# The recurrence of a hybrid encoder layer as one stream per pair of heads, with PSUM laid out by phase

## The chip, the cores and the metric

The kernel runs on one core of a Trainium2 chip. The metric is the device time of one execution in microseconds. The engines are TensorE (PE; its weight loads are shown apart as PEld), VectorE (DVE), ScalarE (ACT), GpSimd (POOL) and SyncE (SP), which issues the DMAs. Each runs its own instructions in order; semaphores order the engines against each other.

## What is computed

One layer of a streaming encoder on 2048 prompt rows and 32 sample rows of 1024 features. After a LayerNorm, one projection yields the inputs of two branches: A, softmax attention over a band of 9 chunks of 64 frames (8 heads of 64), and B, a gated delta rule (8 heads of 64). Both are gated, projected, merged and projected once more, with a LayerNorm at the end. The change lies in branch B. Per head, with chunks of 64 tokens:

```
k_beta = kb * beta                        # a depthwise conv, SiLU and L2 norm stand before
m      = (k_beta kb^T) * decay * strict   # 64 x 64, for each chunk
t_inv  = inverse(eye + m)                 # triangular
u, w   = t_inv (v * beta), t_inv (k_beta * exp(gc))
qk     = (qb kb^T) * decay
for each chunk, in order:                 # the recurrence: s is the 64 x 64 state
    v_new = u - w s
    o     = (q * exp(gc)) s + qk v_new
    s     = s * exp(g_last) + (k * exp(g_last - gc))^T v_new
```

All but the loop can be done for any chunk at any time; the loop is sequential in the chunks of one head and independent from head to head. The sample rows are one more chunk per head, with a state of their own.

## The kernel before

The prompt is done in two halves of 1024 rows. Each half has a phase B (delta rule, function `phase_b`) and a phase A (attention, `phase_a`); the merge of both branches and the output projection come last. Two heads are one *pair* (128 partitions), so there are four pairs; a *block* is 8 chunks of one pair, so each half has 8 blocks (two per pair), and the second half one more for the sample rows.

The program is written out by a small planner (`Flow`). Each piece of work is a Python generator, a *stream*, with a clock of its own. The planner always continues the stream with the earliest clock, writes its next instructions into the engines' queues and moves the clock on by a price for each (`Engine.price`). Buffers are `Gate`s that a stream waits for and gives back. So the order of instructions on each engine is fixed when the program is built, and on the chip each engine works through its queue in that order and waits on semaphores where something is late.

TensorE's main work are the *projection jobs* (`multiply`, PSUM tag `pj`): 128 output columns of the big projection each, as three float16 products per 128 rows of input (`hi` and `lo` parts). They go on through all phases. Their order is a list: `HEAD` jobs for the merge gates, the jobs of phase B (`ORDER`, with `FILL` gate jobs between pairs), six `TAIL` gate jobs, then the jobs of phase A. A job of phase A can begin only when phase B of its half is `done`.

In phase B each block goes through these streams:

- `prep` and `system` (the stream `local` does the blocks in order): decay factors, products `k k^T` and `q k^T`, into block-diagonal tiles `k_bd`, `qk_bd`; 4 slots (`par_slots`).
- `side`: `q_bd`, `kd_bd` and the values by token, `v_t`; 3 slots each (`side_slots`, `vt_slots`).
- `solve` (two of them): 31 steps of forward substitution on VectorE (tiles `sys_t`, `sys_u`), with the data re-laid through DRAM buffers `pd` and `ud`.
- `inverse`: joins the 32 x 32 inverses to the block-diagonal `u_bd` (3 slots, `u_slots`), with one PSUM bank `a` and one `b`. With its two last copies `u_bd<-b` and `u_bd<-a`, and `side` done, the block is `ready`.
- `chain` (lines 1254 to 1293): one stream that does all blocks of the half in order, 8 steps a block. A step is the product of `k_bd` with the state (`xs`), `r` on VectorE, the product with `u_bd` (`ys`), `vn` on VectorE, the product with `kd_bd` (`ds_`), the state's update on VectorE; and for the output (`os_`) the products of `q_bd` with the state and of `qk_bd` with `vn`, copied to `v_t` by ScalarE. It gives back the slots of `par`, `side` and `u` at the block's end.
- `tail`: norm of the output, transposes, gate, to DRAM. It gives `v_t` back. The last tail ends the phase.

PSUM has 8 banks: `pj` 2, `a` 3, `b` 2, `c` 1, for the whole kernel. `chain` takes `a` banks for `xs`, `ys` and `os_` one by one and `c` for `ds_`; `inverse` and `tail` take `a` too.

Of the kernel before, what the change touches and what calls it, by code (L numbers as in the profile page):

```python
# [21 lines left out]
P = 128  # L22
# [8 lines left out]
HD = 64  # L31
# [50 lines left out]
class Gate:  # L82
# [169 lines left out]
def trunk(ctx: ExitStack, tc: tile.TileContext, x_p, x_s, cache_k, cache_v, st_conv, st_gdn,  # L252
# [23 lines left out]

    def mark():
        return Mark(flow)
# [5 lines left out]
    banks = {"pj": 2, "a": 3, "b": 2, "c": 1}  # L284
    bank = {k: gate(n) for k, n in banks.items()}

    def pt(tag):

        return psum.tile([P, 512], F32, tag=tag, bufs=banks[tag], name=tag)
# [449 lines left out]
    def phase_b(half):  # L739

        stack = ExitStack()
        bp = stack.enter_context(tc.tile_pool(name=f"bp{half}", bufs=1, reuse_waits="tile"))
# [28 lines left out]
        pd = [dram.tile([32, 1024], F32, name=f"sol_p{half}{i}") for i in range(NSIDE)]  # L771
        ud = [dram.tile([32, 1024], F32, name=f"sol_u{half}{i}") for i in range(NSIDE)]
# [41 lines left out]
        par_slots, side_slots, u_slots = gate(NPAR), gate(NSIDE), gate(NSIDE)  # L814
        e_slot, tail_slot, p_slots, vt_slots = gate(1), gate(2), gate(NSIDE), gate(NSIDE)
# [177 lines left out]
        def prep():  # L993
            yield decay_done
            for k in order:
# [24 lines left out]
                k.sc = bp.tile([P, 4, 8], F32, tag="sc", bufs=7, name="sc")  # L1020
# [46 lines left out]
        def side(k, ss):  # L1067
# [5 lines left out]
            yield side_slots  # L1073
            k.qb, k.kdb = q_bd[k.n % NSIDE], kd_bd[k.n % NSIDE]
# [27 lines left out]
            yield vt_slots  # L1102
            k.v_t = bp.tile([P, 8, HD], F32, tag="v_t", bufs=NSIDE, name="v_t")
# [17 lines left out]
        def system(k):  # L1121
# [3 lines left out]
            yield par_slots  # L1125
            yield k.qk_ready
            yield k.prep
            yield p_slots
            kb, qkb = k.kb, k.qkb = k_bd[k.n % NPAR], qk_bd[k.n % NPAR]
            p_c = k.p_c = bp.tile([P, 8, HD], F32, tag="p_c", bufs=NSIDE, name="p_c")  # L1130
# [4 lines left out]
            ss = bp.tile([P, 2, 8], F32, tag="ss", bufs=6, name="ss")  # L1135
            k.rr = bp.tile([P, 8], F32, tag="rr", bufs=7, name="rr")
# [28 lines left out]
            dv = pd[k.n % NSIDE][:].rearrange("(c k) (j i) -> k j c i", k=4, i=32)  # L1165
# [6 lines left out]
        def solve():  # L1172
            while True:
# [8 lines left out]
                p0 = pd[k.n % NSIDE][:]  # L1182
# [3 lines left out]
                for g in range(4):  # L1186
                    t = dma(ud[k.n % NSIDE][:].rearrange("s (r g i) -> g s r i", g=4, i=32)[g], sys_u[g * 32:(g + 1) * 32])
# [16 lines left out]
        def inverse(k, t):  # L1204

            yield u_slots
            k.ub = u_bd[k.n % NSIDE]
            nch, ub, p_c = k.nch, k.ub, k.p_c
            u0 = ud[k.n % NSIDE][:]
# [39 lines left out]
            p_slots.give()  # L1249
# [4 lines left out]
        def chain():  # L1254
            for k in order:
                yield k.ready
                sc, v_t = k.sc, k.v_t
                for c in range(k.nch):
                    st = k.state[c]
                    vc = v_t[:, c if k.p is None else c % 4 * 2 + c // 4, :]  # L1260
                    yield bank["a"]
                    xs = pt("a")
                    PE.matmul(xs[:, 0:HD], k.kb[:, c, :], st, start=True, stop=True)
                    yield bank["a"]
                    os_ = pt("a")
                    PE.matmul(os_[:, 0:HD], k.qb[:, c, :], st, start=True, stop=False)
                    flow.cur.last = None
                    r = bp.tile([P, HD], F32, tag="r", bufs=2, name="r")
                    V.scalar_tensor_tensor(out=r[:], in0=xs[:, 0:HD], scalar=k.negc[:, c:c + 1],
                                           in1=vc, op0=ALU.mult, op1=ALU.add)  # L1270
                    bank["a"].give()
                    yield bank["a"]
                    ys = pt("a")
# [955 lines left out]
```

## Time and profile before

| | |
|---|---|
| median of 3 runs | 2184.65 us (2179.92 to 2190.05) |
| the profiled execution | 2182.41 us, span of its instructions 2180.4 us |
| mean granted TensorE clock | 0.965 of 2.4 GHz |
| TensorE busy | 2014.9 us, 92% of the span |
| VectorE, ScalarE, GpSimd busy | 1563.9 us (72%), 1024.8 us (47%), 636.1 us (29%) |

A row of a timeline gives the start and the length of an instruction, or of several of one kind merged, in us from the span's start, then engine, line and operation, the tiles written and read, the shapes and how many; in brackets, how long its engine had been idle and what released it. All instructions are issued in one helper (line 243), so tiles tell them apart: `r<-a,negc,v_t`, for instance, is the step's `r`. A matmul in float32 shows as two records. The recurrence of the first half runs from 216 to 552 us, that of the second from 1044 to 1403.

### The profile page before, as it was taken

Reading aid. Unit: us, or ns where it says so; the run is one execution under the profiler, and the core shown is the slowest. Engines: PE = TensorE matmul, PEld = TensorE weight load, DVE = VectorE, ACT = ScalarE, POOL = GpSimd, SP = SyncE. Lnnn points to the kernel's source line nnn. Section 1 sums busy time; section 2 is a strip of 40 time slices with the busy share of each in tenths; the row PEclk is TensorE's granted clock in tenths of the full one; section 3 lists DMA queues with packets and bytes.
Section 4 is the critical chain, followed back from the end, with each engine's and each line's share of the span. In section 5 each row is a group of like instructions: output and inputs, shape, how many; then the busy total and the mean of one; then the engine's idle time right before and its main releaser. Section 6 shows DMA issues by size and latency. Waiting matters only on the chain. (4 is left out here: it accounts for less than half of the span.)

```text
span 2180.4 us, 41182 instructions
## 1 busy us (share of the span) xinstructions
PE 2014.9 (92%) x15098; PEld 1441.5 (66%) x15098; DVE 1563.9 (72%) x4700; ACT 1024.8 (47%) x2178; POOL 636.1 (29%) x708
## 2 busy tenths in 40 slices
PE   4898998999899999998999999889999998999998
PEld 4454665666455556666777776667676577998896
DVE  7689878873378677679898877447567577676675
ACT  5654545433476677564443533256666652111110
POOL 6343333232212113333223332310110214443333
PEclk9999999999899999999999999999999999999999
DMA  3233232322213113222223223221221325443331
GB/s 119 71 83 104 76 93 53 90 86 83 72 47 102 47 62 111 66 66 66 72 63 98 66 85 89 85 82 41 70 64 47 117 86 192 135 133 110 116 104 59
DMA packets 181718, 185.99 MB, mean 85 GB/s; under 512 B 73862, under 2 KB 131570, under 8 KB 181516
## 3 DMA queue, kind: packets, MB, share of 16 engines
q1 hardware_dynamic: 181516, 183.36, 28.1%
q8 instruction: 119, 1.95, 0.4%
q14 instruction: 83, 0.68, 0.1%
HBM read 135.91 MB, written 50.53 MB: 86 GB/s over the span
## 5 line engine op out<-in xcount | busy, mean ns | idle before, releaser
L243 PE MATMUL pj<-hi,whi 128*128 128x512 f16 (+2 forms) x1992 | 660.1, 346 | 25.6 <-DVE ql L243 7.4
L243 PE MATMUL pj<-hi,wlo 128*128 128x512 f16 (+2 forms) x1952 | 649.8, 345 | 0.9 <-POOL wlo L243 0.9
L243 PEld LDWEIGHTS <-whi 128*128 128x128 f16 x3984 | 412.7, 105 | 230.8 <-issue 17.9
L243 PE MATMUL pj<-lo,whi 128*128 128x512 f16 (+2 forms) x1992 | 458.6, 342 | 0.0
L243 POOL TENSOR_TENSOR wlo<-wraw,whi 128x512 f16<-128x512 f32 x192 | 228.3, 1190 | 702.3 <-ACT whi L243 454.1
L243 PEld LDWEIGHTS <-wlo 128*128 128x128 f16 x1952 | 205.0, 105 | 124.1 <-issue 24.5
L243 ACT CAST mh<-sg 128x256 fp32r<-128x256 f32 x64 | 26.0, 406 | 283.0 <-DVE sg L243 283.0
L243 DVE TENSOR_TENSOR sys_u<-sys_u,sys_t 128x60 f32<-128x60 f32 (+24 forms) x527 | 135.8, 258 | 18.5 <-DVE sys_t L243 0.2
L243 PE MATMUL a<-ghi,whi 128*128 128x256 f32 (+1 forms) x512 | 133.6, 291 | 7.2 <-DVE sg L243 6.9
L243 ACT ACTIVATE wraw<-wraw,w_scale 128x1024 f32<-128x1024 f32 (+1 forms) x98 | 111.4, 1137 | 56.8 <-DVE w_scale L243 56.3
L243 ACT CAST ph<-b 128x512 f16<-128x512 f32 (+2 forms) x224 | 92.4, 421 | 88.2 <-PE b L243 81.5
L243 PE MATMUL a<-ghi,wlo 128*128 128x256 f32 (+1 forms) x512 | 131.8, 288 | 1.0 <-DVE wlo L243 0.9
L243 ACT CAST whi<-wraw 128x512 f16<-128x512 f32 (+1 forms) x196 | 119.6, 611 | 20.2 <-PE pj L243 17.2
L243 ACT ACTIVATE sb<-sb,mx,unit 128x640 f32<-128x640 f32 (+4 forms) x128 | 109.0, 852 | 39.6 <-DVE mx L243 38.8
L243 DVE TENSOR_TENSOR pl<-b,ph 128x512 f16<-128x512 f32 (+2 forms) x224 | 107.2, 485 | 24.1 <-ACT ph L243 22.9
L243 DVE TENSOR_TENSOR sys_t<-sys_u,sys_p 128x60 f32<-128x60 f32 (+21 forms) x459 | 116.3, 253 | 4.7
L243 ACT COPY v_t<-a 128x64 f32<-128x64 f32 x132 | 27.8, 211 | 194.2 <-PE a L243 185.5
L243 DVE SCALAR_TENSOR_TENSOR acc<-raw,cwT,acc 128x512 f32<-128x512 f32 x144 | 113.4, 787 | 6.0 <-ACT acc L243 5.0
L243 POOL TENSOR_TENSOR w_scale<-w_scale,mhalf 128x1 f32<-128x1 f32 x49 | 30.6, 625 | 297.5 <-DVE w_scale L243 233.7
L243 PE MATMUL b<-ident,sb 128*128 128x128 f32 x560 | 100.9, 281 | 7.7 <-ACT sb L243 2.8
L243 PEld LDWEIGHTS a<-ghi,whi 128*128 128x128 f32 x512 | 99.1, 194 | 9.0 <-DVE sg L243 8.3
L243 PEld LDWEIGHTS a<-ghi,wlo 128*128 128x128 f32 x512 | 98.8, 193 | 1.8 <-DVE wlo L243 1.5
(358 smaller groups left out, 4339.1 us busy)
## 6 DMA issues: line engine op xcount, KB each, us to landing
wraw<-in_w_in SPq DMA_DIRECT2D x192, 256.0 KB
sg<-sig SPq DMA_DIRECT2D x112, 128.0 KB
sig<-sig SPq DMA_DIRECT2D x44, 256.0 KB
sys_p<-sol_p SPq DMA_DIRECT2D x17, 512.0 KB
x<-in_x_p SPq DMA_DIRECT2D x16, 512.0 KB
xt<-in_x_p SPq DMA_DIRECT2D x16, 512.0 KB
out_y_p<-xt SPq DMA_DIRECT2D x16, 512.0 KB
glo<-g SPq DMA_DIRECT2D x14, 512.0 KB
```

Source lines behind the costliest of these rows:

```text
L243: r = f(*a, **k)
```

## The change

Each pair's two blocks become a stream of their own, `chain(some)`; the sample block is one more. A stream that has a ready block takes one of two PSUM banks `x` for that block, so that at most two run at a time. All four products of a chunk stand in that bank (64 columns each), those of the next chunk in its other half. The product of `q_bd` with the state moves behind that of `kd_bd`. Since blocks may now end out of order, slots are no longer `k.n % n` but numbers that `Places` hands out and takes back; `p_c` and `v_t` are fixed tiles chosen in that way. The DRAM buffers `pd` and `ud` become eight each, the small tiles `sc`, `ss` and `rr` nine. PSUM keeps `pj` 2 and `b` 2 for the whole kernel; the other four banks are opened by phase: `a` 3 at the start, `a` 2 and `x` 2 in phase B, `a` 3 and `c` 1 in phase A.

```diff
+class Places(Gate):
+    def __init__(self, flow, n):
+        super().__init__(flow, n)
+        self.numbers = deque(range(n))
+    def take(self):
+        yield self
+        return self.numbers.popleft()
+    def back(self, i):
+        self.numbers.append(i)
+        self.give()
...
-    banks = {"pj": 2, "a": 3, "b": 2, "c": 1}
+    banks = {"pj": 2, "b": 2}
     bank = {k: gate(n) for k, n in banks.items()}
+    bank_pool = {k: psum for k in banks}
+    def open_banks(stack, name, **more):
+        pool = stack.enter_context(tc.tile_pool(name=name, bufs=1, space=PSUM, reuse_waits="tile"))
+        for k, n in more.items():
+            banks[k], bank[k], bank_pool[k] = n, gate(n), pool
...
+        open_banks(stack, f"psb{half}", a=2, x=2)
...
-        pd = [dram.tile([32, 1024], F32, name=f"sol_p{half}{i}") for i in range(NSIDE)]
+        pd = [dram.tile([32, 1024], F32, name=f"sol_p{half}{i}") for i in range(2 * NP)]
...
-        par_slots, side_slots, u_slots = gate(NPAR), gate(NSIDE), gate(NSIDE)
-        e_slot, tail_slot, p_slots, vt_slots = gate(1), gate(2), gate(NSIDE), gate(NSIDE)
+        par_slots, side_slots, u_slots, p_slots, vt_slots = (places(n) for n in (NPAR, NSIDE, NSIDE, NSIDE, NSIDE))
+        e_slot, tail_slot = gate(1), gate(2)
...
-            yield side_slots
-            k.qb, k.kdb = q_bd[k.n % NSIDE], kd_bd[k.n % NSIDE]
+            k.sn = yield from side_slots.take()
+            k.qb, k.kdb = q_bd[k.sn], kd_bd[k.sn]
...
-        def chain():
-            for k in order:
+        x_banks = places(2)
+        xb = [pt("x") for _ in range(2)]
+        left = [len(order)]
+
+        def chain(some):
+            for k in some:
                 yield k.ready
+                xn = yield from x_banks.take()
                 sc, v_t = k.sc, k.v_t
                 for c in range(k.nch):
                     st = k.state[c]
                     vc = v_t[:, c if k.p is None else c % 4 * 2 + c // 4, :]
...
+                    xs, os_, ys, ds_ = (xb[xn][:, (c % 2 * 4 + i) * HD:(c % 2 * 4 + i + 1) * HD] for i in range(4))
+                    PE.matmul(xs, k.kb[:, c, :], st, start=True, stop=True)
+                    r = bp.tile([P, HD], F32, tag=f"r{xn}", bufs=2, name="r")
+                    V.scalar_tensor_tensor(out=r[:], in0=xs, scalar=k.negc[:, c:c + 1], in1=vc, op0=ALU.mult, op1=ALU.add)
+                    yield
+                    PE.matmul(ys, k.ub[:, c, :], r[:], start=True, stop=True)
+                    yield
+                    vn = bp.tile([P, HD], F32, tag=f"vn{xn}", bufs=2, name="vn")
+                    V.tensor_scalar(out=vn[:], in0=ys, scalar1=sc[:, 1, c:c + 1], scalar2=None, op0=ALU.mult)
+                    yield
+                    PE.matmul(ds_, k.kdb[:, c, :], vn[:], start=True, stop=True)
+
+                    PE.matmul(os_, k.qb[:, c, :], st, start=True, stop=False)
+                    PE.matmul(os_, k.qkb[:, c, :], vn[:], start=False, stop=True)
+                    V.scalar_tensor_tensor(out=st, in0=st, scalar=sc[:, 3, c:c + 1], in1=ds_, op0=ALU.mult, op1=ALU.add)
+
+                    S.copy(out=vc, in_=os_)
+                    yield
+                x_banks.back(xn)
+                par_slots.back(k.par)
+                side_slots.back(k.sn)
+                u_slots.back(k.un)
                 flow.start(tail(k))
...
-            if k is order[-1]:
+            left[0] -= 1
+            if not left[0]:
                 done.done()
...
-        for g in (worker(todo), worker(decays), prep(), local(), solve(), solve(), chain()):
+        for g in (worker(todo), worker(decays), prep(), local(), solve(), solve()):
             flow.start(g)
+        for some in blocks + ([[sample]] if last else []):
+            flow.start(chain(some))
...
+        open_banks(ctx if half else stack, f"psa{half}", a=3, c=1)
```

## Rows read from the trace of the kernel before

**Rows 1.** The page's first part: busy us, share of the span, instructions.

```profile
PE 2014.9 (92%) x15098; PEld 1441.5 (66%) x15098; DVE 1563.9 (72%) x4700; ACT 1024.8 (47%) x2178; POOL 636.1 (29%) x708
```

**Rows 2.** Windows: length, each engine's busy us, granted clock, DMA share, GB/s.

```profile
216.00:552.00 336.00, 314.53 (x2268) 213.08 (x2268) 251.81 (x924) 151.88 (x314) 101.00 (x124) 0.95 0.29 79
552.00:560.00 8.00, 1.67 (x6) 1.15 (x7) 2.93 (x8) 1.33 (x3) 6.59 (x6) 0.50 0.30 98
```

**Rows 3.** TensorE's groups from 216 to 552: busy us, mean ns, idle before.

```profile
L243 PE MATMUL c<-vn,kd_bd 128*128 128x64 f32 x128 | 25.4, 282 | 9.2 <-DVE vn L243 6.1 <-DVE w_scale L243 3.0
L243 PE MATMUL a<-r,u_bd 128*128 128x64 f32 x128 | 23.9, 269 | 12.2 <-DVE r L243 8.7 <-DVE sys_t L243 2.5 <-ACT zb L243 0.8
...
L243 PE MATMUL a<-state,k_bd 128*128 128x64 f32 x126 | 22.0, 258 | 0.8 <-DVE state L243 0.5
```

**Rows 4.** Timeline of all engines, one step of the last block of the first half.

```profile
533.54 1.15 ACT L243 ACTIVATE wraw<-wraw,w_scale 128x1024 f32<-128x1024 f32 x1
...
534.00 0.33 PE L243 MATMUL a<-state,k_bd 128*128 128x64 f32 x2
...
534.16 0.38 PE L243 MATMUL pj<-hi,wlo 128*128 128x512 f16 x1
...
535.96 0.39 PE L243 MATMUL a<-vn,qk_bd 128*128 128x64 f32 x2
...
536.16 0.28 DVE L243 SCALAR_TENSOR_TENSOR state<-state,sc,c 128x64 f32<-128x64 f32 x1 [0.53 <-PE c L243]
...
536.38 0.21 ACT L243 COPY v_t<-a 128x64 f32<-128x64 f32 x1 [1.04 <-PE a L243]
...
537.04 0.33 PE L243 MATMUL a<-state,k_bd 128*128 128x64 f32 x2
```

**Rows 5.** Timeline of VectorE: the first `r` of blocks 2 to 7, first half.

```profile
307.83 0.28 DVE L243 SCALAR_TENSOR_TENSOR r<-a,negc,v_t 128x64 f32<-128x64 f32 x1 [0.38 <-PE a L243]
...
362.09 0.28 DVE L243 SCALAR_TENSOR_TENSOR r<-a,negc,v_t 128x64 f32<-128x64 f32 x1
...
408.93 0.28 DVE L243 SCALAR_TENSOR_TENSOR r<-a,negc,v_t 128x64 f32<-128x64 f32 x1
...
452.74 0.28 DVE L243 SCALAR_TENSOR_TENSOR r<-a,negc,v_t 128x64 f32<-128x64 f32 x1
...
496.44 0.28 DVE L243 SCALAR_TENSOR_TENSOR r<-a,negc,v_t 128x64 f32<-128x64 f32 x1 [0.69 <-PE a L243]
...
527.68 0.28 DVE L243 SCALAR_TENSOR_TENSOR r<-a,negc,v_t 128x64 f32<-128x64 f32 x1 [0.97 <-PE a L243]
```

**Rows 6.** Timeline of ScalarE: the last `u_bd` copy of blocks 2, 4 and 6.

```profile
297.48 0.36 ACT L243 COPY u_bd<-a 32x256 f32<-32x256 f32 x1
...
391.22 0.36 ACT L243 COPY u_bd<-a 32x256 f32<-32x256 f32 x1
...
490.72 0.36 ACT L243 COPY u_bd<-a 32x256 f32<-32x256 f32 x1 [0.31 <-PE a L243]
```

**Rows 7.** Timeline of VectorE: the first write to `q_bd` of block 5.

```profile
362.29 0.67 DVE L243 TENSOR_TENSOR q_bd<-qk,ex 64x512 f32<-64x512 f32 x1
```

**Rows 8.** Timelines of ScalarE and VectorE: a block of the second half, ready and begun.

```profile
1328.19 0.36 ACT L243 COPY u_bd<-a 32x256 f32<-32x256 f32 x1 [0.31 <-PE a L243]
...
1330.60 0.28 DVE L243 SCALAR_TENSOR_TENSOR r<-a,negc,v_t 128x64 f32<-128x64 f32 x1
```

**Rows 9.** Timeline of TensorE at the end of the first half's phase B.

```profile
545.77 1.03 PE L243 MATMUL pj<-lo,whi 128*128 128x512 f16 x4
...
551.30 0.64 PE L243 MATMUL a<-vn,qk_bd 128*128 128x64 f32 x2
558.33 1.11 PE L243 MATMUL a<-ident,v_t 128*128 128x128 f32 x4 [6.39 <-POOL v_t L243]
559.23 0.63 PE L243 MATMUL pj<-hi,whi 128*128 128x512 f16 x1
559.66 0.63 PE L243 MATMUL pj<-hi,wlo 128*128 128x512 f16 x1
```

More of the change, by code (lines that the diff above doesn't have):

```diff
@@ L275, in gate, with places @@
         return Gate(flow, n)
+    def places(n):
+        return Places(flow, n)
     def mark():
@@ L769, in phase_b @@
         q_bd, kd_bd, u_bd = (diag(n, NSIDE) for n in ("q_bd", "kd_bd", "u_bd"))
[L771 to L772 removed]
+        pd = [dram.tile([32, 1024], F32, name=f"sol_p{half}{i}") for i in range(2 * NP)]
+        ud = [dram.tile([32, 1024], F32, name=f"sol_u{half}{i}") for i in range(2 * NP)]
+        p_cs, v_ts = ([bp.tile([P, 8, HD], F32, name=f"{x}{i}") for i in range(NSIDE)] for x in ("p_c", "v_t"))
         col = bp.tile([P, 2, NP, nch_all], F32, name="col")
@@ L1101, in side @@
             yield from by_token(k.qk[:, 1, :], nch, put_k)
-            yield vt_slots
-            k.v_t = bp.tile([P, 8, HD], F32, tag="v_t", bufs=NSIDE, name="v_t")
+            k.vn = yield from vt_slots.take()
+            k.v_t = v_ts[k.vn]
             yield bank["b"]
@@ L1124, in system @@
             n = nch * CH
-            yield par_slots
+            k.par = yield from par_slots.take()
             yield k.qk_ready
             yield k.prep
-            yield p_slots
-            kb, qkb = k.kb, k.qkb = k_bd[k.n % NPAR], qk_bd[k.n % NPAR]
-            p_c = k.p_c = bp.tile([P, 8, HD], F32, tag="p_c", bufs=NSIDE, name="p_c")
+            k.pn = yield from p_slots.take()
+            kb, qkb = k.kb, k.qkb = k_bd[k.par], qk_bd[k.par]
+            p_c = k.p_c = p_cs[k.pn]
             qk, e_in, sc = k.qk, k.e_in, k.sc
@@ L1204, in inverse @@
         def inverse(k, t):
-            yield u_slots
-            k.ub = u_bd[k.n % NSIDE]
+            k.un = yield from u_slots.take()
+            k.ub = u_bd[k.un]
             nch, ub, p_c = k.nch, k.ub, k.p_c
-            u0 = ud[k.n % NSIDE][:]
+            u0 = ud[k.n % (2 * NP)][:]
             yield t
@@ L1269, in chain @@
[L1269 to L1273, printed above, removed]
-                    PE.matmul(ys[:, 0:HD], k.ub[:, c, :], r[:], start=True, stop=True)
+                    xs, os_, ys, ds_ = (xb[xn][:, (c % 2 * 4 + i) * HD:(c % 2 * 4 + i + 1) * HD] for i in range(4))
+                    PE.matmul(xs, k.kb[:, c, :], st, start=True, stop=True)
@@ L1279, in chain @@
                     yield
-                    yield bank["c"]
-                    ds_ = pt("c")
-                    PE.matmul(ds_[:, 0:HD], k.kdb[:, c, :], vn[:], start=True, stop=True)
-                    PE.matmul(os_[:, 0:HD], k.qkb[:, c, :], vn[:], start=False, stop=True)
-                    V.scalar_tensor_tensor(out=st, in0=st, scalar=sc[:, 3, c:c + 1], in1=ds_[:, 0:HD],
-                                           op0=ALU.mult, op1=ALU.add)
-                    bank["c"].give()
-                    S.copy(out=vc, in_=os_[:, 0:HD])
@@ L1360, in tail @@
                 yield t
-            vt_slots.give()
+            vt_slots.back(k.vn)
             if k.p is None:
```

34 lines of the change are left out of this document (11 added, 23 removed).

## The prediction

> **What bounds the kernel now.** I read the busy shares first, then windows by phase, then the instructions of the recurrence, then the chain of readiness around it, last the two phase ends. TensorE is busy for 92% of the span [rows 1], so a change that takes no matmul away can win only what TensorE loses by waiting or by running at its lower clock. The windows say where that is [rows 2]: in the recurrence of the first half (216 to 552) TensorE is busy 314.5 of 336 us with a granted clock of 0.95, and VectorE 251.8; in the 8 us behind it TensorE works 1.7 us and the granted clock is 0.50, the lower level, 1.2 GHz. The idle time that stands before the recurrence's matmuls is in the grouped rows [rows 3]: 9.2, 12.2 and 0.8 us in the first half, 22.2 together. So the stake is some 20 us of waits in each half and the hole at a phase's end, not the length of the recurrence as such: while the recurrence waits, projection matmuls run.
>
> One step of the recurrence is to be seen in [rows 4]: the product of `k_bd` with the state at 534.00, that of `qk_bd` with `vn` at 535.96, the state update 536.16, the copy of the output 536.38, the next step 537.04. That is 3.0 us with little beside it. Beside other work it is far longer: blocks of 8 steps begin at 307.83, 362.09, 408.93, 452.74, 496.44 and 527.68 [rows 5], so they take 54, 47, 44, 44 and 31 us.
>
> When is a block ready? Its last `u_bd` copy ends at 297.84, 391.58 and 491.08 for the blocks whose first `r` comes at 307.83, 408.93 and 496.44 [rows 5, 6]: 10, 17 and 5 us of waiting for the one recurrence stream. So in the first half the stream is late, and it also holds back what comes later: with three side slots, `q_bd` of block 5 is written at 362.29, just after block 2 ends (its successor's `r` is at 362.09) [rows 5, 7], and from there to the readiness of block 6 (491.08) it takes 129 us.
>
> In the second half it is otherwise [rows 8]: a block ready at 1328.55 starts at 1330.60. The eight others wait between 0.4 and 5.2 us. There the stream follows its inputs.
>
> **The change part by part.**
>
> *Two streams, one per pair.* The two blocks of a pair share a state and stay in sequence, so only the second block of one pair and the first of the next can overlap. With two streams an even block of the first half starts some 2 us after it is ready. Block 2: 300, with its own length of 54 us it ends at 354 in place of 362. So block 3 starts 8 us earlier and `q_bd` of block 5 is written 8 us earlier, which makes block 6 ready at 483 instead of 491; it starts at 485, 11 us earlier. But now it runs beside block 5 for some of its time: with 31 us (its old length) it ends at 516, with 44 us (that of block 5) at 529, no earlier than before (527.7). Block 7 follows. So the recurrence ends 0 to 12 us earlier than the 551.94 at which the last output product ends [rows 9]; I take 9.
>
> What that is worth is read at the end of the phase [rows 9]. The last projection matmuls of the phase run until about 546.8; then TensorE has two recurrence steps (until 551.94), waits 6.4 us for `v_t` of the last tail, transposes it, and starts the next phase's projections at 559.23, first at 0.63 us each where 0.38 is usual. 12.4 us lie between the last projection and the next, of which steps and transposes need about 3 (two steps of five products and four transposes). With the recurrence ending 9 us earlier those projections and the tail lie beside each other and the hole mostly closes: 9 us, and the slow start after it, some ten matmuls that begin 0.43 us apart (559.23, 559.66) instead of 0.22 (the four from 545.77 on take 1.03, one alone 0.38), 2 us more. I take -11, with ends 0 (the projections end later by as much) and -12.
>
> In the second half nothing starts earlier by the second stream, since each block starts when it is ready [rows 8]. End to end 0 to -8 (the hole after the phase, like that in [rows 9]); taken: 0.
>
> *Own banks.* Before, recurrence, inverse and tail share three `a` banks, and the recurrence holds two. After, it has two banks `x` and never asks; inverse and tail have two `a`. No row prices a bank wait alone. Bounds: nothing, and 1 us for each of 17 blocks; the steps in which an inverse runs beside the recurrence are long for other reasons too (VectorE is 75% busy [rows 2]), so I take the low side, -2 in all.
>
> *One bank for four products, and the new order in a step.* The product of `q_bd` with the state moves from before `r` to behind the product of `kd_bd`, next to that of `qk_bd`. Instruction counts stay. Three things follow. First, the cover between the state's product and that of `u_bd` is gone by one matmul (0.16 us from one start to the next, 534.00 to 534.16 [rows 4]), and `r` has to come sooner. Second, in [rows 4] the state update (536.16) runs while the product of `qk_bd` (535.96 to 536.35) still does. They write and read different banks there. In one bank I take it that the update comes after both output products: 536.35, 0.16 for the moved one and 0.04 to the update make 536.55, 0.39 later; and that the copy comes after the update. Third, the next step's first product then waits for the copy: 0.39 later, 0.04 + 0.21 for the copy and 0.06 to the matmul make 0.70 us behind the old end of the update (536.44), against 0.60 us at which it comes now (537.04) [rows 4] (the 0.04 and 0.06 are estimates: the copy starts at 536.38, 0.03 after the product that it waits for ends). So a step in the open grows by 0.1 us, and loses up to 0.16 where the moved product had held up TensorE. Over 132 steps that is -21 to +13; where ScalarE is in a long instruction (1.15 us for a weight's scaling [rows 4]) the copy comes later, and the upper bound is 0.25 us a step, +33. Most steps are not in the open: they stand between other work. I take +3.
>
> The Trainium skill speaks against this part: PSUM — Partial Sum Buffer, section "PSUM bank collisions raise a hardware error", says that two of TensorE, VectorE and ScalarE may not touch the same bank and quadrant at once, different columns or not, so accesses have to be kept apart by bank. By that rule the term is the one above, +3; if addresses alone counted, update and copy could run as before, and it would be about -1.
>
> *Shared waits.* Where two streams run at once a matmul of one fills a wait of the other. By the times above they overlap for three stretches of some 10 us among 336; of the 22.2 us of waits [rows 3] that is 2. Bounds 0 and -22 (-44 if the second half, whose waits I take to be alike, did the same); taken -2.
>
> *Places, larger small tiles, eight DRAM buffers, banks by phase.* No instruction is added. Buffers in the order in which they come free can only let a block start sooner; a phase's new banks wait for the old phase's last readers, which [rows 9] shows finished before the next projections. Nothing; hidden by the hole at the phase's end, a microsecond each if that hole closes (three boundaries).
>
> **Sum.** -11 - 2 + 3 - 2 = -12. The profiled execution took 2182.4 us, 2.0 of it around its span; 2170.4 after. The median of the runs is 2.2 us above that execution, so I predict 2172.6 us, 0.55% less.
>
> **The rivals.**
>
> *The projections set the phase's length (no change).* If TensorE, with 314.5 of 336 us busy [rows 2], is the limit, an earlier end of the recurrence only moves projections behind it. For it: the hole of 12.4 us contains no projection because there were none left, so the work before it was just enough. Against it: the 22 us of waits. Time 2182, within 3.
>
> *The shared bank holds the step up (slower).* Each step's copy on ScalarE now stands between two steps, behind ScalarE's queue, and TensorE, which runs in order, waits at the next step's first product with all projections behind it. ScalarE is 45% busy in that stretch [rows 2]. At 0.25 us a step, 132 steps cost 33; with the -11 and -2 of the first parts, 2182.4 + 20 + 2.2 = 2205. It decides from about 0.1 us of stall a step (13 us), where it eats the gain. Beside it stands the page named above.
>
> *The streams overlap far more (much faster).* If slots given back out of order let blocks become ready sooner than my loop of 129 us, half of the 22 us of waits in each half and the hole go, with 8 us at the end of the second half: 2182.4 - 22 - 11 - 8 + 3 + 2.2, so 2147. Against it: VectorE's 75%, which the solve shares.
>
> **How the numbers follow.** Chances: forecast 0.36, no change 0.30, slower 0.20, much faster 0.14. A measurement can tell about 0.5% from no change (11 us): faster is below 2173.7, slower above 2195.6. The forecast lies just inside faster, and I give it 0.27 of its 0.36 there and 0.09 to the same; of no change 0.27 is the same and 0.03 slower. Faster 0.41, same 0.36, slower 0.23. The range takes in the much faster and the slower case nearly to their own times, 2145 to 2204; the forecast alone runs from 2163 (all holes closed) to 2180 (half of term one).
>
> **What would show it.** Right: the last output product of the first half ends near 543, the next phase's projections begin near 549 with no 6 us before the transposes; first `r` of even blocks within 2 us of their `u_bd`; the second half's ends unchanged. Wrong: idle time before the products with the state, now 0.8 us in the first half [rows 3], grows above 5 us, with ScalarE's copy as releaser; or the hole stands where it was; or two streams run side by side through most of the phase.

## The result, and the profile after

The kernel after takes 2192.51 us (median of 17 runs, 2176.67 to 2199.07), the kernel before in the same comparison 2184.49 (17 runs): a ratio of 1.0032, 95% interval 1.0019 to 1.0045, 7 us slower. The forecast was 2172.6, faster. A second measurement of the same kernel (e18 below) gave 1.0029, 1.0007 to 1.0051.

The page's first part of the kernel after (compare [rows 1]):

```profile
PE 2033.5 (93%) x15098; PEld 1429.5 (65%) x15098; DVE 1567.5 (72%) x4700; ACT 1022.6 (47%) x2178; POOL 633.7 (29%) x708
```

The instruction counts are the same on every engine; TensorE is busy 18.6 us longer with them. The windows of the kernel after (columns as in [rows 2]):

```profile
216.00:552.00 336.00, 317.62 (x2236) 203.09 (x2236) 255.22 (x918) 146.95 (x308) 100.14 (x122) 0.95 0.28 76
552.00:560.00 8.00, 6.71 (x36) 3.50 (x36) 1.72 (x8) 2.95 (x6) 2.69 (x2) 1.00 0.41 131
360.00:400.00 40.00, 36.44 (x233) 25.87 (x232) 28.31 (x96) 16.27 (x33) 8.68 (x10) 0.70 0.09 25
```

The hole that the prediction aimed at is closed: from 552 to 560 TensorE works 6.71 us at full clock, where it had worked 1.67 at half [rows 2]. But in the 336 us before it does 32 instructions fewer in 3 us more of busy time, and there is a new place, 360 to 400, with a mean granted clock of 0.70.

TensorE's timeline at the end of the first half (after; compare [rows 9]):

```profile
552.50 0.39 PE L259 MATMUL x<-vn,qk_bd 128*128 128x64 f32 x2
...
556.39 1.89 PE L259 MATMUL pj<-lo,whi 128*128 128x512 f16 x8
559.57 0.38 PE L259 MATMUL b<-w_sq,tiny 128*128 128x1 f32 x2 [1.29 <-ACT whi L259]
559.82 0.64 PE L259 MATMUL a<-ident,v_t 128*128 128x128 f32 x4
560.29 0.38 PE L259 MATMUL pj<-hi,whi 128*128 128x512 f16 x1
```

Projections now run from the last output product to the tail's transposes, without the 6.39 us before these; the next ones follow 0.22 us apart, at full clock. Yet the last output product comes at 552.50, 1.2 us later than before, and was forecast near 543. So the recurrence didn't get shorter: projections that had been done earlier are left over to fill the hole.

A block's readiness (timelines of ScalarE and VectorE, after): the last `u_bd` copy of block 2, then its first `r`.

```profile
308.47 0.36 ACT L259 COPY u_bd<-a 32x256 f32<-32x256 f32 x1
...
311.37 0.28 DVE L259 SCALAR_TENSOR_TENSOR r<-x,negc,v_t 128x64 f32<-128x64 f32 x1
```

The wait of block 2 fell from 10 us to 2.5, as forecast for the even blocks, but the block was ready 11 us later than in [rows 6], so it starts 3.5 us later. The delay goes with the late `q_bd` product and not with the second stream: of the kernels below, e2, e3 and e5, which have it late, show block 2 ready at 308 to 312 us, and e4, with two streams and the product early, at 299.

One step in the kernel after, between other work (timeline, all engines; TensorE's weight loads left out):

```profile
355.80 0.28 DVE L259 TENSOR_SCALAR vn<-x,sc 128x64 f32<-128x64 f32 x1
...
356.14 0.43 PE L259 MATMUL x<-vn,kd_bd 128*128 128x64 f32 x2
...
356.41 0.39 PE L259 MATMUL x<-state,q_bd 128*128 128x64 f32 x2
...
356.63 0.39 PE L259 MATMUL x<-vn,qk_bd 128*128 128x64 f32 x2
...
356.86 0.38 PE L259 MATMUL pj<-hi,wlo 128*128 128x512 f16 x1
...
357.20 0.27 DVE L259 SCALAR_TENSOR_TENSOR state<-state,sc,x 128x64 f32<-128x64 f32 x1
...
357.51 0.21 ACT L259 COPY v_t<-x 128x64 f32<-128x64 f32 x1 [1.46 <-DVE state L259]
...
357.94 0.33 PE L259 MATMUL x<-state,k_bd 128*128 128x64 f32 x2
```

Two things are to be seen. The three products stand in one go and take 0.72 us, 0.22 of it for the moved one, where a product beside projections took 0.16 [rows 4]. And the state update comes after the `qk_bd` product, the copy after the update, the next `k_bd` product after the copy: the four products' users take turns. Over all steps 185.5 us of the copy's idle time were ended by TensorE's product in before, and 260.8 us are ended by `state` in the kernel after (one row of each profile, before first):

```profile
L243 ACT COPY v_t<-a 128x64 f32<-128x64 f32 x132 | 27.8, 211 | 194.2 <-PE a L243 185.5
L259 ACT COPY v_t<-x 128x64 f32<-128x64 f32 x132 | 28.0, 212 | 268.9 <-DVE state L259 260.8
```

That users of one bank have to be kept apart is what the prediction took from the Trainium skill (PSUM — Partial Sum Buffer, "PSUM bank collisions raise a hardware error"). The trace agrees in that the copy now waits for the update's semaphore, with the 260.8 us above.

TensorE's groups from 216 to 552 (after; columns as in [rows 3]):

```profile
L259 PE MATMUL x<-r,u_bd 128*128 128x64 f32 x128 | 26.8, 293 | 12.1 <-DVE r L259 10.4 <-DVE ms L259 1.4
L259 PE MATMUL x<-vn,kd_bd 128*128 128x64 f32 x126 | 25.9, 289 | 5.5 <-DVE vn L259 5.3
L259 PE MATMUL x<-state,q_bd 128*128 128x64 f32 x126 | 25.3, 284 | 0.0
...
L259 PE MATMUL x<-state,k_bd 128*128 128x64 f32 x126 | 23.5, 270 | 2.0 <-ACT v_t L259 2.0
```

Idle time is 19.6 us where it was 22.2 [rows 3]: waits alone don't show the loss. The products themselves are longer: `u_bd` 293 ns where 269 stood, `k_bd` 270 where 258 stood.

### The profile page after: what moved, and what is told of

The parts are those of the page before. It is cut to its first block, busy times and chain, and to the rows that moved or that the text cites. A ratio compares the mean times of both kernels' runs of the same rounds, so it can differ in the third digit from the quotient of the medians.

```text
span 2191.6 us, 41057 instructions
## 1 busy us (share of the span) xinstructions
PE 2033.5 (93%) x15098; PEld 1429.5 (65%) x15098; DVE 1567.5 (72%) x4700; ACT 1022.6 (47%) x2178; POOL 633.7 (29%) x708
## 5 line engine op out<-in xcount | busy, mean ns | idle before, releaser
L259 PEld LDWEIGHTS <-whi 128*128 128x128 f16 x3984 | 404.3, 103 | 228.0 <-issue 12.3
L259 PE MATMUL pj<-lo,whi 128*128 128x512 f16 (+2 forms) x1992 | 447.4, 340 | 0.0
L259 ACT COPY v_t<-x 128x64 f32<-128x64 f32 x132 | 28.0, 212 | 268.9 <-DVE state L259 260.8
L259 DVE TENSOR_TENSOR sys_t<-sys_u,sys_p 128x60 f32<-128x60 f32 (+21 forms) x459 | 121.7, 265 | 4.1
```

Of the source, the lines that this page charges most:

```text
L259: r = f(*a, **k)
```

## The experiments

The change does three things to the recurrence at once: two streams, another order in the step (the `q_bd` product late), one bank for four products. Three theories: the loss is in the streams (S), in the order (called P for the three products in one go, O for the order as a whole, C for the cover that `r` loses) or in the bank (B). Each edit also changes the order in which the planner writes all other work, so a run tests a part of the change together with the order that goes with it. Beside each median stands the ratio to the kernel before, measured on the same chip; before's medians were 2182.8 to 2184.6.

**One stream or two, old step or new.** e1: the kernel after with `yield` between the three products.

```
 PE.matmul(ds_, k.kdb[:, c, :], vn[:], start=True, stop=True)
+yield
 PE.matmul(os_, k.qb[:, c, :], st, start=True, stop=False)
+yield
 PE.matmul(os_, k.qkb[:, c, :], vn[:], start=False, stop=True)
```

> The kernel after, with the planner free to put other work between the kd_bd, the q_bd and the qk_bd product of a step (in the program 111 of the 132 kd_bd products are now followed by a projection matmul; after: none). Theory P (packing): three float32 products back to back leave their weight loads uncovered, about 0.06 us a step more than before, 132 x 0.06 = 8 us: 2184 us, a ratio to before of 0.998 to 1.001. Theory B (one bank): the products, the state update and the copy of a step take turns in one bank, and that is the loss: the state update now waits for two projection matmuls more, some 0.45 us a step, so no better than after, 2192 to 2205 us. Theory S (two streams): the other order of work around two streams is the loss: 2192 us, as after.

2179.48 us, 0.9979 (0.9964 to 0.9994): at the fast end of what P gave, and not what B or S gave.

e2: one stream, with the new step and its bank.

```
-for some in blocks + ([[sample]] if last else []):
-    flow.start(chain(some))
+flow.start(chain(order))
```

> The kernel after, with one stream over all blocks in the order of before (the step, its two banks and the numbered places stay). Theories P and B: the loss is in the step, so about as slow as after or slower, since the holes at the ends of the two phases come back (some 5 us each): 2192 to 2200 us. Theory S: about as before, 2182 to 2187 us.

2184.87 us, 1.0009 (0.9991 to 1.0026): the time that S gives. But P and B had counted on the holes at the phases' ends, and the first half's did not come back (from 540 to 556 TensorE is busy 15.5 us at full clock).

e3: the kernel before with its `q_bd` product moved, and with it the request for the bank that it writes.

```
-yield bank["a"]
-os_ = pt("a")
-PE.matmul(os_[:, 0:HD], k.qb[:, c, :], st, start=True, stop=False)
 ...
+yield bank["a"]
+os_ = pt("a")
 PE.matmul(ds_[:, 0:HD], k.kdb[:, c, :], vn[:], start=True, stop=True)
+PE.matmul(os_[:, 0:HD], k.qb[:, c, :], st, start=True, stop=False)
 PE.matmul(os_[:, 0:HD], k.qkb[:, c, :], vn[:], start=False, stop=True)
```

> The kernel before, with the q_bd product moved behind the kd_bd product, each product still in a bank of its own and one stream. Theory P: the three products stand back to back (128 of 132 in the program), 8 us lost: 2190 to 2194 us. Theory B: nothing shares a bank, so about as before, 2183 to 2187 us. Theory S: as before, 2183 to 2187 us.

2178.60 us, 0.9978 (0.9959 to 0.9998): faster, which no theory had said.

e4: the kernel after with before's step and banks; two streams stay.

```
-open_banks(stack, f"psb{half}", a=2, x=2)
+open_banks(stack, f"psb{half}", a=3, c=1)
 ...
+the step of before: xs, os_, ys from tag a, ds_ from tag c, q_bd product behind the k_bd product
```

> The kernel after with its two streams, but the step and the banks of before (three banks of tag a and one of tag c, q_bd product behind the k_bd product). Theory P and theory B: none of the loss, and the ends of the phases are filled as in after: 2176 to 2184 us. Theory S: as after or worse, 2192 to 2200 us.

2163.24 us, 0.9913 (0.9892 to 0.9933), faster than any of the theories had it. So two streams alone gain 19 us, and S falls. Windows of the stretch from 330 to 500 and of the end of the first half, before first:

```profile
330.00:500.00 170.00, 157.95 (x1165) 107.34 (x1164) 136.65 (x506) 75.21 (x156) 51.78 (x64) 0.94 0.27 73
...
540.00:556.00 16.00, 10.66 (x64) 7.61 (x61) 6.21 (x22) 5.55 (x12) 3.55 (x4) 0.82 0.31 88
```

The same windows of e4:

```profile
330.00:500.00 170.00, 161.00 (x1223) 106.74 (x1222) 142.39 (x522) 80.08 (x167) 57.90 (x69) 1.00 0.31 87
...
540.00:556.00 16.00, 9.77 (x33) 6.00 (x34) 3.84 (x14) 1.78 (x5) 8.77 (x8) 0.54 0.29 83
```

In the same 170 us e4's TensorE does 1223 instructions for 1165, and its clock stays at 2.4 GHz throughout (1.00 for 0.94). The hole at the phase's end stands in e4 as in before: two streams don't close it.

**Order against bank, and the hole.** e5: e4 with the `q_bd` product moved as in e3.

> Two streams and a bank of its own for each product (as in e4_two_old), with the q_bd product moved behind the kd_bd product (as in the kernel after): between e4_two_old and the kernel after stand now the order in the step and the shared bank, and this run changes the order alone. Theory O (order: in the traces so far the three kernels with q_bd, kd_bd and qk_bd in one go spend 17 to 21 us more of TensorE around the step's products outside the stretches of low clock, and e4_two_old 1 us more): 2178 to 2186 us. Theory B (bank): as e4_two_old, 2161 to 2168 us.

2193.82 us, 1.0043 (1.0027 to 1.0059). Own banks, and all of the loss: the order, at a higher price than theory O gave. The kernel after differs from e5 by the shared bank alone, and its ratio (1.0032, 1.0019 to 1.0045) is no higher.

e6: the kernel after with the product back in its place, its output from tag `a`; three products stay in the stream's bank.

```
 PE.matmul(xs, k.kb[:, c, :], st, start=True, stop=True)
+yield bank["a"]
+os_ = pt("a")[:, 0:HD]
+PE.matmul(os_, k.qb[:, c, :], st, start=True, stop=False)
 ...
-PE.matmul(os_, k.qb[:, c, :], st, start=True, stop=False)
```

> The kernel after, with the q_bd product back behind the k_bd product and its output in a bank of tag a; the other three products of a step stay in the stream's one bank, and the two streams stay. Theory O: the order was the loss, so 2163 to 2174 us. Theory B: the three products left in one bank still take turns (the state update no longer waits for the qk_bd product), so most of the loss stays: 2182 to 2193 us.

2166.39 us, 0.9933 (0.9910 to 0.9956): in the range of O.

e7 and e8: e4 and the kernel before with one projection job more held back for the end of the first half.

```
-HEAD, TAIL = [2, 3], [6, 6]
+HEAD, TAIL = [2, 3], [7, 6]
```

> e4_two_old with one projection job more (seven where six were) held back for the end of the first half. In e4_two_old's profile TensorE runs out of projections at 537 us and its clock is at 1.2 GHz for 17.1 us from 537.8. If that hole is the price: a job of some 10 us fills it, 5 to 9 us faster than e4_two_old, 2154 to 2160 us. If the work is only moved, and the hole comes back in another place: as e4_two_old, 2161 to 2167 us.

> The kernel before with the same one job more at the end of the first half, where its TensorE is nearly idle from 550 to 560 us at 1.2 GHz. It tells what that hole alone is worth (the prediction gave it 11 us for both halves): 2174 to 2179 us if the hole is filled, 2182 to 2186 us if the work is only moved.

e7: 2156.59 us, 0.9886 (0.9866 to 0.9905). e8: 2171.75 us, 0.9949 (0.9932 to 0.9966). The hole is worth 6 us to e4 and 11 us to the kernel before. The end of the first half in e7 and in e8:

```profile
540.00:556.00 16.00, 14.71 (x82) 8.20 (x81) 5.55 (x24) 8.17 (x14) 6.11 (x6) 1.00 0.26 88
```

```profile
540.00:556.00 16.00, 16.00 (x103) 11.13 (x102) 5.88 (x24) 5.72 (x13) 1.97 (x3) 1.00 0.29 83
```

Where before had worked 10.66 us at a clock of 0.82, both work nearly all 16 us at full clock.

e12: e6 with the same job more.

> e6_two_one_early (the kernel after with the q_bd product back behind the k_bd product, its output in a bank of tag a) with one projection job more at the end of the first half, as in e7_two_old_tail. If the shared bank costs nothing: as e7_two_old_tail, 2154 to 2161 us. If three products taking turns in one bank cost something that the hole hid: 2163 to 2170 us.

2157.43 us, 0.9887 (0.9865 to 0.9909): as e7. Three products in one bank cost nothing that can be measured.

e11: e5 with the same job more.

> e5_two_own_late with one projection job more held back for the end of the first half, as in e7_two_old_tail. With e7 and e8 it makes the same three cases without the hole there. If hole and order add up: 7 to 11 us less than e5_two_own_late, 2182 to 2187 us, still some 27 us above e7_two_old_tail. If the hole is what the new order costs two streams: 2160 to 2172 us.

2180.79 us, 0.9993 (0.9978 to 1.0007). Hole and order add up: without the hole the new order costs 24 us (e11 less e7; 23 by the ratios). The windows from 1100 to 1380, in the second half, of before, e7, e11 and the kernel after, one each:

```profile
1100.00:1380.00 280.00, 264.12 (x2243) 200.06 (x2241) 224.90 (x806) 117.71 (x266) 83.09 (x105) 0.97 0.31 83
```

```profile
1100.00:1380.00 280.00, 267.15 (x2287) 203.15 (x2286) 218.24 (x783) 117.39 (x272) 83.52 (x105) 0.97 0.29 81
```

```profile
1100.00:1380.00 280.00, 261.47 (x2169) 193.08 (x2168) 215.34 (x772) 112.17 (x258) 78.76 (x100) 0.96 0.29 78
```

```profile
1100.00:1380.00 280.00, 259.84 (x2133) 187.92 (x2133) 222.28 (x793) 112.49 (x257) 78.69 (x103) 0.96 0.28 76
```

At nearly the same clock TensorE gets through 2243 instructions with one stream, 2287 with two, and 2169 or 2133 when the `q_bd` product is late, own banks or not.

**What of the order costs.** e9: e4 with the `q_bd` product behind the `u_bd` product, alone between projections; e15: the same with the job more.

> e4_two_old (two streams, a bank of its own for each product) with the q_bd product moved behind the u_bd product: it then stands alone between projection matmuls, as in e4_two_old, but no longer between the k_bd and the u_bd product. In the program the k_bd and the u_bd product are 4.4 matmuls apart, 6.4 in e4_two_old and 4.0 in the kernel after. Theory C (cover: the u_bd product now comes up on TensorE before VectorE has written r, in some 60% of the steps against 33% before, and that is the price of the new order): 2176 to 2190 us. Theory P (packing: three float32 products in one go with bare weight loads are the price): 2161 to 2170 us.

> e9_q_mid with one projection job more at the end of the first half, so that it stands beside e7_two_old_tail (2156.6 us) and e11_own_late_tail (2180.8 us) without the hole. Here the q_bd product stands alone but behind the u_bd product. Theory C: most of the 24 us between the two stays, 2168 to 2178 us. Theory P: most is gone, 2156 to 2163 us.

e9: 2177.79 us, 0.9967 (0.9953 to 0.9981). e15: 2169.30 us, 0.9941 (0.9919 to 0.9963). About half of the cost is there as soon as the product no longer stands between `k_bd` and `u_bd` (12.7 of 24 us, e15 less e7). Both times lie in the range of theory C.

e10: e5 with e1's two `yield`s; e14: the same with the job more; e17: with two jobs more (`FILL = [1, 2, 2, 1]`, `TAIL = [7, 5]`).

> e5_two_own_late (two streams, own banks, q_bd product behind the kd_bd product) with the planner free to put other work between the three products, so that they no longer stand in one go (114 of 132 kd_bd products are followed by a projection matmul). Theory C: r is no sooner, 2182 to 2194 us. Theory P: 2163 to 2175 us.

> e10_own_late_yields with one projection job more at the end of the first half. In e10's profile TensorE runs out of projections at 535 us, with the recurrence alone until 573 us at 1.2 GHz for 41.0 us, so that its 2188 us don't tell what the three products in one go cost. Theory C (the late q_bd product leaves r uncovered): the hole shrinks by one job and 10 to 14 us go, 2172 to 2180 us, as far from e7_two_old_tail as e11_own_late_tail is. Theory P (packing): 2158 to 2168 us.

> e10_own_late_yields with two projection jobs more in the first half (one among its heads' jobs, one at its end; in the second half one job only moves from its end to the middle). e14's one job left a hole of 20.5 us at 1.2 GHz at the end of the first half, so its 2178 us don't decide. In the second half e10 and e14 take 407 us from the first to the last projection where the three kernels with two streams and the products in one go take 420 to 423 and those with the q_bd product in its old place 403 to 408. Theory P (the three products in one go are the price): 2158 to 2168 us once the hole is closed. Theory C (r uncovered): 2172 to 2181 us.

e10: 2187.73 us, 1.0020 (1.0008 to 1.0032). e14: 2178.25 us, 0.9975 (0.9957 to 0.9992). e17: 2179.63 us, 0.9993 (0.9970 to 1.0015). All three times lie in the ranges of theory C. Spreading gives 1 to 6 us in the total (13 in the shared bank, e1). In e10 the recurrence runs on almost alone from 535 to 573 us:

```profile
535.00:573.00 38.00, 25.07 (x120) 20.77 (x120) 10.17 (x40) 6.51 (x17) 6.97 (x7) 0.53 0.14 42
```

So in e10 the loss has turned into a hole, and e14 kept half of it. e17 closed it, but took 16 us more in the second half (table below), where one of its gate jobs also moved from the end to the middle. The second half in windows, e10 first, then e17:

```profile
1024.00:1430.00 406.00, 376.44 (x3181) 280.27 (x3179) 319.57 (x1124) 171.84 (x391) 119.69 (x156) 0.97 0.30 83
1001.00:1423.00 422.00, 389.94 (x3182) 287.79 (x3180) 321.31 (x1124) 172.73 (x391) 122.08 (x156) 0.94 0.29 79
```

The work is the same, the clock is not: e17 was at 1.2 GHz for 51.2 us, e10 for 20.5 (from the traces' clock rows). Half of the difference is 15 us, so most of the 16 us is the price of the lower clock.

e13: the kernel after with 0.5 us more allowed for `r` when the order is written; e16: the same with two jobs more (`TAIL = [8, 6]`).

```
 V.scalar_tensor_tensor(out=r[:], in0=xs, ...)
+flow.cur.clock += 0.5
```

> The kernel after with 0.5 us more allowed for r when the program's order is written, so that the u_bd product comes later on TensorE: 6.1 matmuls lie between the k_bd and the u_bd product (4.0 in the kernel after, 6.1 in the kernel before). The order of a step's products, the one bank and the two streams stay. Theory C: most of the loss is gone, 2170 to 2182 us. Theory P: 2187 to 2193 us, as after.

> e13_after_cover with two projection jobs more at the end of the first half. In e13's profile the u_bd product's wait for r is nearly gone (27.8 to 10.8 us in both halves), half of that came back before the kd_bd product (20.8 to 31.7 us), and TensorE had no projections left from 534 us to 569 us, 34.1 us of it at 1.2 GHz; projections had been 28 us ahead of the kernel after's at that point. If the hole ate what the cover gave: 20 to 25 us less than e13, 2178 to 2183 us, and so 10 to 14 us below the kernel after. If the longer step itself is the loss: 2192 to 2200 us.

e13: 2203.21 us, 1.0092 (1.0077 to 1.0107), slower than either theory had it. e16: 2184.26 us, 1.0004 (0.9990 to 1.0019). TensorE's groups of e16 from 1044 to 1404, with the mean ns and the idle time before:

```profile
L259 PE MATMUL x<-vn,kd_bd 128*128 128x64 f32 x130 | 27.0, 290 | 11.0 <-DVE vn L259 10.7
...
L259 PE MATMUL x<-r,u_bd 128*128 128x64 f32 x130 | 23.0, 260 | 6.1 <-DVE r L259 6.0
```

The same groups of the kernel after:

```profile
L259 PE MATMUL x<-r,u_bd 128*128 128x64 f32 x130 | 27.3, 293 | 10.6 <-DVE r L259 6.4 <-DVE ms L259 1.5 <-ACT raws L259 1.4
L259 PE MATMUL x<-vn,kd_bd 128*128 128x64 f32 x130 | 26.7, 288 | 6.7 <-DVE vn L259 6.4
```

Room before `u_bd` takes its wait from 10.6 to 6.1 us and the product from 293 to 260 ns, but 4.3 us of wait come back one product on, before `kd_bd`. And the step is longer: in e13 the projections ran out and a hole of 34 us at 1.2 GHz ate more than the cover gave; with it closed, e16 is 6 us below the kernel after by the ratios, 8 by the medians. The table below has that gain in the first half alone, where e16 has two jobs more and no stretch at 1.2 GHz near 370.

e18: the kernel after once more.

> The kernel after, unchanged, a second time, for its profile: in the first one TensorE waited 2.6 us for r at 366.9 us and then stayed at 1.2 GHz for 23.9 us, the longest such stretch inside a phase. If that stretch belongs to the kernel's order of work it stands in this profile too, at 365 to 375 us and over 15 us long (e2_one_stream has one of 23.9 us at 371.6). If it was chance: no stretch over 11 us there, and a span some 8 us shorter. The time: 2188 to 2196 us.

2191.53 us. The clock's stretch stands there again (23.9 us from 369.9), in this window of e18:

```profile
360.00:400.00 40.00, 36.44 (x231) 25.39 (x230) 28.45 (x97) 16.29 (x33) 8.20 (x12) 0.70 0.13 31
```

What comes ahead of it (timeline of the kernel after, TensorE and VectorE):

```profile
366.10 0.81 PE L259 MATMUL pj<-lo,whi 128*128 128x512 f16 x3
366.50 1.22 DVE L259 TENSOR_TENSOR sys_u<-sys_u,sys_t 128x52 f32<-128x52 f32 x1
...
368.13 0.74 DVE L259 SCALAR_TENSOR_TENSOR acc<-raw,cwT,acc 128x512 f32<-128x512 f32 x1
...
369.15 0.28 DVE L259 SCALAR_TENSOR_TENSOR r<-x,negc,v_t 128x64 f32<-128x64 f32 x1
...
369.48 0.69 PE L259 MATMUL x<-r,u_bd 128*128 128x64 f32 x2 [2.56 <-DVE r L259]
```

`r` stands behind the solve and the convolution on VectorE; TensorE waits 2.56 us for it, and its clock falls. One step of the solve alone, at 366.50, took 1.22 us (see the last section).

**Both halves side by side.** This is counted from the traces' start times: the projections' matmuls are the same in all kernels, so the time from No. 672 (at 224.8 us in before) to No. 3168 (1008.7) holds the first half's recurrence and its end, that from No. 3168 to No. 4700 the second half's. The rest of a span, 980 to 989 us, stands in neither column. The two columns are of the one profiled execution of each kernel (e6's took 11 us more than the median of its runs, the others differ from theirs by 5 at most), the ratio is of all its runs.

```
kernel            streams  q_bd product  output's bank  first  second   ratio
before               1     early         own            783.8   413.3   1
e8  (+1 job)         1     early         own            776.6   412.8   0.9949
e3                   1     late          own            768.2   423.1   0.9978
e2                   1     late          shared         777.3   425.1   1.0009
e4                   2     early         own            773.6   407.6   0.9913
e7  (+1 job)         2     early         own            766.5   404.1   0.9886
e6                   2     early         own, 3 share   783.5   406.3   0.9933
e12 (+1 job)         2     early         own, 3 share   769.9   403.1   0.9887
e9                   2     behind u_bd   own            773.1   415.3   0.9967
e15 (+1 job)         2     behind u_bd   own            768.2   414.5   0.9941
e5                   2     late          own            780.9   422.9   1.0043
e11 (+1 job)         2     late          own            771.3   420.2   0.9993
e1                   2     late, spread  shared         787.1   414.0   0.9979
e10                  2     late, spread  own            798.7   407.0   1.0020
e14 (+1 job)         2     late, spread  own            786.4   406.5   0.9975
e17 (+2 jobs)        2     late, spread  own            774.8   423.0   0.9993
after                2     late          shared         785.7   423.1   1.0032
after again (e18)    2     late          shared         781.3   423.6   1.0029
e13                  2     late, room    shared         790.0   426.5   1.0092
e16 (+2 jobs)        2     late, room    shared         770.2   425.8   1.0004
```

"3 share": the other three products share the stream's bank. The second half is the clean one: 413 us with one stream and the product early, 403 to 408 with two; 420 to 427 wherever it is late and in one go; 414 and 415 behind `u_bd`; 407 to 423 late and spread. The first half hangs on how the projections and the recurrence come out together at its end.

The clock blurs the second half too. At 1.2 GHz projections follow each other 0.43 us apart where 0.22 is usual [rows 9], so a microsecond of work there costs half a microsecond. Taking off half of the time in which TensorE was at the lower clock and not idle (from the same traces) leaves, as an estimate: 395 and 396 us with one stream and the product early, 385 to 393 with two; 398 and 399 behind `u_bd`; 397 to 400 spread, e17 with them; 404 to 410 late and in one go, with one stream or two, with room or without. Kernels whose programs differ only in the first half lie within 4 us of each other. So the `q_bd` product's leaving its place costs some 7 us (e9 and e15 against e4 and e7), and its standing in one go with the other two some 8 us more (e5 and e11).

## Why the prediction was wrong

From before to after in four steps of the runs, by their ratios times 2184: two streams -19 (e4), the hole closed -6 (e7), the late `q_bd` product +23 (e11), all four products in one bank +9 (after against e11). That is the +7 measured. Another path through the runs has the same ends: two streams -19 (e4), the late product +28 (e5), one bank -2 (after), with the hole closing in the last step. The forecast had the same parts, with other sizes.

- *One bank and the new order, +3*, is the step that failed; it measured +32 (+26 on the second path, where the closed hole is part of it). Its bounds (-21 to +33) held the value, and the choice of the low side was wrong. It was priced as the latency of a lone step, 0.1 us. What the runs show is a price in the rate at which TensorE gets through its instructions: 2169 where 2287 were done in 280 us, with the order alone changed (e11, e7). The prediction named the lost cover (one matmul, 0.16 us a step) and left it out because most steps stand between other work. In the written program the cover shrank by more: 6.1 matmuls stood between the `k_bd` and the `u_bd` product in before, 4.0 in after.
- *Of the 32, the bank.* The turns in the bank came as described. Three products share it for nothing (e12 as e7). All four, with the late product, cost 7 to 9 us on the first path (e2 less e3, after less e11) and nothing on the second (after less e5). The 7 to 9 us stand mostly in the first half, and there in the clock: e2 and after were at 1.2 GHz for 44.4 and 54.6 us, e3 and e11 for 20.5 each, and in e2 and after alone the clock falls for 23.9 us near 370. That the bank makes that stall, rather than the written order that goes with it, was not tested.
- *Of the 32, the order.* Some half is the product's leaving its place between `k_bd` and `u_bd` (e15), the rest its going behind `kd_bd`. By the second half, with the clock taken off, the uncovered place and the three products in one go each have a part: the product alone behind `u_bd` costs some 7 us, all three in one go some 8 more, and spreading them gives those back (e10, e14 and e17 as e9 and e15). That is an estimate from one execution of each. In the totals the spread kernels with own banks fall by 1 to 6 us only, for they end in a hole or, in e17, spend more time at the lower clock. Room before `u_bd` gives 6 to 8 us in the total (e16), but most of its wait returns before `kd_bd`, and in the second half the time is 2 to 3 us longer with it and the estimate 4 to 6 us shorter, hardly more than its scatter.
- *Own banks, -2.* No run takes this term alone. e12, with a bank for three products of the recurrence, takes as long as e7 without.
- *Shared waits, -2*, was mis-sized: two streams alone gave 19 us, near the 22 that the rival of far more overlap took for them. Of the earlier blocks that this rival took, only the last shows clearly: in e4 block 7 was ready 11 us earlier than in before and block 6 2 us earlier, block 2 1 us and block 4 4 us later. They gave a full clock from 330 to 500 and, in the second half, where 0 was taken, 6 to 9 us. With the late product that gain is gone: e2 with one stream and the kernel after with two take 425 and 423 us there.
- *The end-of-phase hole, -11*, closed as forecast, but not by the second stream. In e4, which has the two streams without the late product, the recurrence did end 7 us earlier (544.7), near the 9 that was taken, and the hole stays: the projections end earlier too. With one stream and the late product (e3) the first half is 16 us shorter and has no hole. It is a matter of which runs out first, and one job more closes it (e8: -11 us, the forecast's size).
- *The slower rival* (the shared bank holds TensorE at the next step's first product) had the direction, and a wrong mechanism: idle time before `k_bd` products grew to 2.0 us, not above 5. The range reached up to 2204 for its sake alone, so that it held the measured time was luck. *The rival of unchanged length* was right that TensorE sets it.

The best version is e7, or e12 with the change's bank for three products: 1.1% under the kernel before.

## What to carry to other kernels

Where an in-order TensorE fills a recurrence's waits with other matmuls, price a moved product by the cover that it takes from the next wait and by the products that it then stands beside, times the number of steps, and not by the latency of a step in the open. When a change has several parts, run each alone: here one part's gain of 19 us lay under another's loss of 32. And when a stall inside a phase goes, look at the phase's end, for the work that it covered may now run out too soon; a job moved there is a cheap test.

## What was not expected of the hardware

- After the wait of 2.56 us the granted clock stayed at 1.2 GHz for 23.9 us, in both profiles of the kernel after, although TensorE was busy 3.47 to 4.00 of each 4 us from 370 on (3.00 to 4.00 in e18). From one start to the next that wait took 2.9 us; in the kernel before, 2.2 us for `r` (at 232) and 3.4 us for `vn` (at 315) were followed by 3.4 and 6.8 us at 1.2 GHz. What makes the difference was not tested.
- A float32 product that TensorE has to wait for is longer itself. In the kernel before, at full clock in both recurrences, the first record of a `u_bd` product took 305 ns on average in the 26 with idle time before them and 241 ns in the other 101. In the kernel after the 102 without such time took 294 as well, so the idle time shown is not the whole of it; what makes those longer was not tested.
- The subtraction on 128x52 at 366.50 took 1.22 us, that on 128x50 at 368.00 took 0.21. GpSimd was in a tensor operation of its own (`wlo`) from 366.49 to 367.65. That is a pattern: in the kernel after, all 63 steps of the solve with two tensor inputs (`sys_u`, `sys_t`) that took more than 0.6 us ran for most of their time beside a GpSimd operation (44 beside `wlo`), and of the 716 without one beside them none took more than 0.24 us; e18 shows 64 and 716, before 54 and 723. No run moved the GpSimd work, so what it would give is open.
